# Fifteen seven-product pairs in each half of a down projection, with one weight sum of each fresh pair formed by GpSimd

## The chip, the core and the metric

The kernel runs on one core of one Trainium2 chip. The time is the device time of one execution in microseconds (us). Five engines work side by side, each on its own list of instructions in a fixed order: TensorE (PE in the profile), VectorE (DVE), ScalarE (ACT), GpSimd (POOL) and SyncE (SP), whose list here holds transfers only. GpSimd's list holds both computing and the start of transfers. An instruction that waits holds up everything behind it on its own list.

## The reference, cut to what matters

```python
def reference(x, ...):                       # x: (1, 256, 2048) float32, one layer
    x = mixer_block(x, ...)                  # gated token mixer, unchanged by this edit
    x = conv_ffn(x, norm_ffn, w_up, conv_k, conv_b, w_down)
    return rms_norm(x, norm_final)

def conv_ffn(x, g_norm, w_up, conv_k, conv_b, w_down):
    up = rms_norm(x, g_norm) @ w_up          # 2048 -> 2 x 5504 columns
    up = ...                                 # width-3 convolution over positions
    gate, val = jnp.split(up, 2, axis=-1)
    return x + (jax.nn.silu(gate) * val) @ w_down   # 5504 -> 2048: the down projection
```

The edit concerns the last product, a (256 x 5504) matrix times a (5504 x 2048) matrix, and a little of the final norm.

## The kernel before, in words

**Precision.** A float32 number is used as a high part plus a low part. Each product of two blocks is three matmuls: high x high, low x high, high x low. The function `triple` issues them on lines 323, 324 and 325, in this order. The high part of a weight block is made by ScalarE (`whi`, line 176), the low part by VectorE (`wlo`, line 177), both from the raw block that a transfer brought (`wraw`, five buffers, issued on SyncE's list from line 148). `whi` and `wlo` have four buffers each.

**Tiling of the down projection.** The 2048 output columns are done in two halves of 1024, which the text calls the first and the second half. In each half the 5504 inner rows are 43 blocks of 128, so 21 pairs of blocks and one single block. One block times 1024 columns is a piece. The 256 positions are two halves of 128, the columns of a piece two halves of 512, and a pair therefore is a 2 x 2 block product: eight triples, or, by the Strassen-Winograd scheme, seven. The list `DOWN_PAIRS` names the pairs of rows that go the second way, and `DOWN_QUADS` the places (0 to 20) in each half's order at which they stand. The text calls these places q0 to q20; place q has pieces 2q and 2q+1. There are three kinds of pair:

- a plain pair: eight triples on the split raw blocks, four per piece;
- a fresh pair: seven triples, three in its first piece and four in its second. Its second piece needs four sums of raw weight blocks, in the tiles t13 and t24 (two sums each), and their high and low parts h13, l13, h24, l24. They are made on the spot: `weight_sums` forms the sums on VectorE (lines 366, 367, 369, 370), and `weight_sums_split` the parts (line 380 on ScalarE, line 381 on VectorE). Each tile exists once, so a pair's parts can be written only when TensorE has done with those of the fresh pair before;
- a read pair (`DOWN_SPLIT`, five of the list): seven triples, whose parts were made and written to DRAM during the up projection by `split_ahead`, and are read back (`split_read`, line 1274) on GpSimd's list into tiles of the pool "twice".

Both kinds of seven-product pair also need sums of activations. They are formed during the up projection (`sums`, `sums_split` in `ev_up`, lines 1113 to 1117), written to DRAM, and read back by `stored` (line 1420) on GpSimd's list into three tiles in turn; each read waits until TensorE has done with the pair three places earlier in that turn.

**Order of the work.** `begin(i)` stands ahead of the matmuls of piece i. It issues loads up to piece i+4, splits up to piece i+3, and runs what `at(i, ...)` put there: for a fresh pair at piece i the sums at i-3 and their parts at i-2. So VectorE and ScalarE run up to three pieces ahead of TensorE, and the buffers hold them there.

**The end.** The last four pieces of the second half are done block by block of the output (`finish`), so that the norm of one block overlaps the products of the next. `ev_sums` adds the seven-product terms to the residual stream a little earlier; its last two adds are lines 1010 and 1011.

In the trace all of t13, t24, h13, h24, l13, l24 and two of the three tiles of `stored` have the name h, and the third has the name s; ff's activations are a. TensorE's weight side and moving side are both listed, so `bank<-h,h` is a product with sums of weights.

Of the kernel before, what the change touches and what calls it, by code (L numbers as in the profile page):

```python
# [69 lines left out]
PAD = 16  # L70
DOWN_PAIRS = (2, 3, 5, 6, 7, 9, 10, 11, 13, 14, 15, 16, 17, 18)
DOWN_QUADS = ((1, 3, 5, 6, 7, 9, 10, 11, 13, 14, 15, 17, 18, 19), (1, 2, 4, 5, 6, 8, 9, 10, 12, 13, 14, 16, 17, 18))
DOWN_SPLIT = (2, 6, 10, 14, 17)
DOWN_JOBS = ((0, 2), (4, 6), (8, 10), (12, 14), (16, 18))
DOWN_LEADS = ({2: (4, 16, 16), 3: (5,), 5: (8,), 6: (7, 8, 8)}, {})
TWICE_AT = -15
SCALE_AT = (14, 15, 22, 23)
FIN_AT = 36


@with_exitstack
def trunk_kernel(ctx, tc, x, x_t, vecs, w_in, ln_g, ln_b, w_st, b_s, rpb, w_branch, w_out, w_up, w_down,
# [108 lines left out]

    tasks = {}
    preload = {}

# [94 lines left out]

    def wide(src, row0, order, c0, acts, quads, room, done, sums=None, stored=None, split=None, late=False, lead=4, behind=(), ahead={}):  # L290
        n0 = plan_wide(src, row0, order, c0)
        boxes = {}
        for q in quads:
            i = n0 + 2 * q
            k = order[2 * q]
            units[i], units[i + 1] = 1, 2
            b = boxes[q] = {}
            ready = split[0].get(k // 2) if split else None
            if stored:
                b["acts"] = {}  # L300
                at(i - (ready[0] if ready else ahead.get(k // 2, lead)), lambda b=b, k=k: stored(k // 2, b["acts"]))
            else:
                b["acts"] = sums[k]
            if ready:
# [4 lines left out]
            whole[i] = whole[i + 1] = None  # L309
            halves = late and q == quads[0]  # L310
# [48 lines left out]

    def weight_sums(i, box, room, halves=False):  # L360
        r0, r1 = whole.pop(i), whole.pop(i + 1)
# [7 lines left out]
        nc.vector.tensor_add(t13[:, 0], r0[:, 0], r0[:, 1])  # L369
        nc.vector.tensor_add(t13[:, 1], r0[:, 1], r1[:, 1])  # L370
        if halves:
# [3 lines left out]

    def weight_sums_split(box, room):
        u = []
        for name, t in zip(("13", "24"), box.pop("w")):
            h, l = room("h" + name, F32R), room("l" + name, F32R)
            nc.scalar.activation(h, t, AF.Copy)  # L380
            nc.vector.tensor_sub(l, t, h.bitcast(F32))
            u.append((h, l))
        split_sums(box, u)

# [4 lines left out]
    def run_wide(g, tail=0):  # L389
# [20 lines left out]
        for i in range(n0, n1 - tail):  # L410
# [30 lines left out]
            if sp:  # L441
                done[0](P, i)
        if not tail:
            done[1](C, n1)
            return
# [544 lines left out]

    def ev_sums(j, room):
        def done(P, i):
# [172 lines left out]
    def finish(ps, t, c):  # L1165
        x2 = rs["x2"]
        last = t == NT - 1 and c == 1
        if c == 0:
            fin["y", t] = hpool.tile([128, 2, 512], F32, name=f"h{t}")
        y, g = fin["y", t], fin["g", 2 + c]  # L1170
        if last:
            square_columns(t, 2 + c, ps[t][c])
        else:
            add_down(ps[t][c], t, 2 + c)
            square_columns(t, 2 + c)
            nc.vector.tensor_mul(y[:, c], columns_of(t, 2 + c), g)
        if c == 0:
            if t:
                fin["out"]()
            else:  # L1180
                p = ps[NT - 1][1]
                nc.vector.tensor_add(p, p, columns_of(NT - 1, 3))
# [240 lines left out]

    def down_split_tile(pair, name):
        return ff["twice"].tile([128, 2, 512], F32R, name=name)

    d_kept = {}

    def down_order(g):
# [4 lines left out]

    g_dn = [wide(w_d, 0, down_order(g), g * 1024, lambda k: ff["a"][k], DOWN_QUADS[g], down_room,
                 (ev_sums(2 * g, down_room), ev_down if g == 0 else finish), stored=stored,
                 ahead={p: n[0] for p, n in DOWN_LEADS[g].items()},
                 split=({p: DOWN_LEADS[g].get(p, (6, 6)) for p in DOWN_SPLIT}, split_read(d_kept, g, down_split_tile))) for g in range(2)]
    ff["kept"] = {p: dram.tile([128, 2, 384], F32, name=f"sums{p}") for p in DOWN_PAIRS}
# [120 lines left out]

    at(g_dn[0][1] + TWICE_AT, open_twice)
    at(g_dn[0][1] + 3, open_third)
    for g in g_up:
        run_group(g)

    def open_fin():
        fc["st"].close()
        fin["p"], fin_st = pool("fin", "right")
# [4 lines left out]
    fin["ss"] = const.tile([128, NT, 4], F32, name="ss_3")  # L1573
    at(g_dn[0][1] + FIN_AT, open_fin)
    def load_fin():
# [49 lines left out]
```

## Time and profile before

| | |
|---|---|
| time, median of 3 runs | 1286.87 us (1286.46 to 1287.11) |
| the profiled execution | 1286.83 us |
| its span, first to last instruction | 1285.0 us, so 1.8 us lie around it |
| granted TensorE clock, mean | 0.998 |
| busy: TensorE, VectorE, ScalarE, GpSimd | 99%, 88%, 62%, 14% of the span |
| the down projection's products | 1061 to 1276.6 us of the span |

The profiled execution stands 0.04 us below the median, well inside the runs' spread of 0.65 us. TensorE's busy time is made of matmuls whose ends are modelled, so 99% says that it never lacked work for long, and nothing of how fast it worked; for that the starts of successive matmuls have to be looked at.

### The profile page before, as it was taken

What the parts mean: (1) busy time and instruction counts of PE and PEld (TensorE: products, weight loads), DVE (VectorE), ACT (ScalarE), POOL (GpSimd) and SP (SyncE); (2) the same over time, 40 slices, a digit from 0 to 9 for tenths busy, and PEclk for the clock granted to TensorE, in tenths of its full rate; (3) what the DMA queues carried; (4) which work ended last, traced back from release to release, by engine and by line L of the source; (5) the groups of instructions that cost most, each with busy time, mean ns of one, the idle gap of its engine ahead of it and who ended that gap; (6) DMA issues with size and microseconds to landing.
All of it is one profiled execution on the core that took longest, in us unless ns stands there. A gap on an engine that the chain in (4) does not pass through costs nothing.

```text
span 1285.0 us, 19798 instructions
## 1 busy us (share of the span) xinstructions
PE 1275.2 (99%) x6711; PEld 1088.0 (85%) x6711; DVE 1128.0 (88%) x1675; ACT 795.9 (62%) x1198; POOL 174.4 (14%) x328
## 2 busy tenths in 40 slices
PE   9999999999999999999999999999999999999997
PEld 7888888888888888888888888888888888888886
DVE  7898977777799988897989999899999989989988
ACT  7776575775755555566656666566566656555554
POOL 0003842330000001100000010011001001211210
PEclk9999999999999999999999999999999999999999
DMA  9779889989789967965878888888788779998993
GB/s 365 279 271 278 289 270 345 333 288 323 255 310 368 351 234 255 390 219 180 278 239 258 298 268 259 280 287 273 247 300 290 250 252 341 359 384 337 370 373 144
DMA packets 200485, 375.54 MB, mean 292 GB/s; under 512 B 16320, under 2 KB 124480, under 8 KB 200384
## 3 DMA queue, kind: packets, MB, share of 16 engines
q1 hardware_dynamic: 175472, 285.84, 64.1%
q0 software_dynamic: 24480, 87.78, 19.5%
q8 instruction: 52, 0.85, 0.3%
q10 hardware_dynamic: 432, 0.66, 0.1%
q14 instruction: 49, 0.40, 0.1%
HBM read 323.63 MB, written 48.50 MB: 290 GB/s over the span
## 4 chain that ended last, share of the span: by engine, by line
PE 96%; DVE 2%; DMA 1%; issue 0%; ACT 0%; DVEq 0%; SPq 0%; ACTq 0%
PE bank L228 31%; PE bank L232 16%; PE bank L323 11%; PE bank L325 11%; PE bank L324 11%; PE bank L256 5%; PE bank L257 5%; PE bank L258 5%; DMA wraw<-in_w_down_dram 1%; DVE wlo L177 0%; PE bank L877 0%; PE bank L831 0%; PE bank L504 0%; PE bank L866 0%; PE bank L704 0%
## 5 line engine op out<-in xcount | busy, mean ns | idle before, releaser
L177 DVE TENSOR_TENSOR wlo<-wraw,whi 128x1024 fp32r<-128x1024 f32 (+1 forms) x471 | 534.8, 1150 | 113.1 <-ACT whi L176 73.8
L176 ACT ACTIVATE whi<-wraw 128x1024 fp32r<-128x1024 f32 (+1 forms) x471 | 460.3, 993 | 219.3 <-PE bank L324 65.4
L228 PE MATMUL bank<-h,whi 128*128 128x512 f32 x1760 | 423.3, 391 | 0.0
L228 PEld LDWEIGHTS bank<-h,whi 128*128 128x128 f32 x1760 | 322.8, 188 | 62.0
L232 PEld LDWEIGHTS bank<-h,wlo 128*128 128x128 f32 x1760 | 225.9, 191 | 8.7
L232 PE MATMUL bank<-h,wlo 128*128 128x256 f32 x1760 | 228.6, 283 | 0.0
L1088 ACT ACTIVATE tc<-ta,ck 128x256 f32<-128x256 f32 x86 | 47.1, 595 | 106.6 <-DVE ta L1086 106.6
L325 PE MATMUL bank<-wlo,a 128*128 128x512 f32 x200 | 78.0, 390 | 0.0
L324 PE MATMUL bank<-whi,a 128*128 128x512 f32 x200 | 77.8, 389 | 0.0
L323 PE MATMUL bank<-whi,a 128*128 128x512 f32 x200 | 77.8, 389 | 0.0
L323 PE MATMUL bank<-whi,h 128*128 128x512 f32 x168 | 66.0, 393 | 0.0
L324 PE MATMUL bank<-whi,h 128*128 128x512 f32 x168 | 65.6, 390 | 0.0
L325 PE MATMUL bank<-wlo,h 128*128 128x512 f32 x168 | 65.5, 390 | 0.0
L1091 DVE SCALAR_TENSOR_TENSOR tc<-ta,ck,tc 128x255 f32<-128x255 f32 x86 | 41.4, 482 | 14.4 <-ACT tc L1088 14.4
L1314 DVE TENSOR_TENSOR tw<-tw 128x512 f32<-128x512 f32 x72 | 50.3, 699 | 0.7
L256 PE MATMUL bank<-whi,h 128*128 128x512 f32 x128 | 50.3, 393 | 0.0
L256 PE MATMUL bank<-whi,y 128*128 128x512 f32 x128 | 50.3, 393 | 0.0
L257 PE MATMUL bank<-whi,h 128*128 128x512 f32 x128 | 49.8, 389 | 0.0
L257 PE MATMUL bank<-whi,y 128*128 128x512 f32 x128 | 49.8, 389 | 0.0
L258 PE MATMUL bank<-wlo,h 128*128 128x512 f32 x128 | 49.8, 389 | 0.0
L258 PE MATMUL bank<-wlo,y 128*128 128x512 f32 x128 | 49.8, 389 | 0.0
L380 ACT ACTIVATE h<-h 128x1024 fp32r<-128x1024 f32 x36 | 38.0, 1057 | 16.5 <-DVE h L370 13.7
(329 smaller groups left out, 1988.8 us busy)
## 6 DMA issues: line engine op xcount, KB each, us to landing
wraw<-in_w_up_dram SPq DMA_DIRECT2D x336, 256.0 KB, 4.2
wraw<-in_w_in_dram SPq DMA_DIRECT2D x107, 512.0 KB, 6.3
wraw<-in_w_down_dram SPq DMA_DIRECT2D x76, 512.0 KB, 7.5
wraw<-in_w_in_dram SPq DMA_DIRECT2D x70, 256.0 KB, 4.4
wraw<-in_w_branch_dram SPq DMA_DIRECT2D x32, 512.0 KB, 5.4
wraw<-in_w_out_dram SPq DMA_DIRECT2D x28, 512.0 KB, 6.8
tw<-in_w_down_dram POOLq DMA_DIRECT2D x10, 1024.0 KB, 8.0
down_h<-so POOLq DMA_DIRECT2D x20, 512.0 KB, 3.7
```

The source lines that it names most:

```text
L176: nc.scalar.activation(h[:, k, :m], w[:, k, :m], AF.Copy)
L177: nc.vector.tensor_sub(l[:, k, :m], w[:, k, :m], h[:, k, :m].bitcast(F32))
L228: nc.tensor.matmul(p, h[:, k - k0, b * 128:(b + 1) * 128], acts(k), start=k == 0, stop=k == nk - 1)
L232: nc.tensor.matmul(p[:, :T], l[:, k - k0, b * 128:(b + 1) * 128], acts(k)[:, 0, :], start=False, stop=False)
L256: nc.tensor.matmul(p, xh, h[:, kk, :m], start=st, stop=False)
L257: nc.tensor.matmul(p, xl, h[:, kk, :m], start=False, stop=False)
L258: nc.tensor.matmul(p, xh, l[:, kk, :m], start=False, stop=sp)
L323: nc.tensor.matmul(p, xh, h, start=st, stop=False, **kw)
L324: nc.tensor.matmul(p, xl, h, start=False, stop=False, **kw)
L325: nc.tensor.matmul(p, xh, l, start=False, stop=sp, **kw)
L1088: nc.scalar.activation(v, u, AF.Identity, scale=ck[:, 1, ch:ch + 1], bias=ck[:, 3, ch:ch + 1])
L1314: nc.vector.tensor_add(w[:, d], w[:, a], w[:, b])
```

## The change

The list of seven-product pairs grows from fourteen to fifteen (pair 12 is new), in both halves. Pair 11 takes the place of pair 10 among the five that are read; so ten pairs instead of nine are fresh in each half. With fewer plain pairs to stand between, two fresh pairs follow each other directly at two places of each half: q9 and q10, q16 and q17 in the first; q8 and q9, q15 and q16 in the second. For the second pair of three of these four (`DOWN_BESIDE`) h13 and l13 get tiles of their own, in a pool opened where the convolution's was, or in activation tiles that the second half no longer needs (`DOWN_FREED`); the rest of their parts, and at q17 of the first half all of them, are issued behind the products of the piece before (`after`). Pair 17's h13 and l13 are read into such tiles too.

In the down projection `weight_sums` now gives the sum t13[:, 1] of each fresh pair to GpSimd. The last two adds of the second half's `ev_sums` move into `finish`. The pool for the final norm opens 49 - 36 = 13 pieces later (the first half has 43 pieces, and it now opens at piece 6 of the second), and two scalings move from pieces 22 and 23 to 24 and 25.

```diff
-DOWN_PAIRS = (2, 3, 5, 6, 7, 9, 10, 11, 13, 14, 15, 16, 17, 18)
+DOWN_PAIRS = (2, 3, 5, 6, 7, 9, 10, 11, 12, 13, 14, 15, 16, 17, 18)
...
-DOWN_SPLIT = (2, 6, 10, 14, 17)
+DOWN_SPLIT = (2, 6, 11, 14, 17)
...
+DOWN_BESIDE = ((10,), (9, 16))
+DOWN_FREED = ((0, 2), (1, 3))
...
-            at(i - 3, lambda i=i, b=b, halves=halves: weight_sums(i, b, room, halves))
+            at(i - 3, lambda i=i, b=b, halves=halves: weight_sums(i, b, room, halves, nc.gpsimd if helped else nc.vector))
...
+            if q in beside:
+                at(i - 2, lambda b=b, q=q: weight_sums_split(b, room, (0,), beside[q]))
+                after[i - 1] = lambda b=b: weight_sums_split(b, room, (1,))
+                continue
+            if q - 1 in made:
+                after[i - 1] = lambda b=b: weight_sums_split(b, room)
+                continue
...
         nc.vector.tensor_add(t13[:, 0], r0[:, 0], r0[:, 1])
-        nc.vector.tensor_add(t13[:, 1], r0[:, 1], r1[:, 1])
+        second.tensor_add(t13[:, 1], r0[:, 1], r1[:, 1])
...
             def second_half():
                 nc.vector.tensor_sub(x12, x12, m["v"])
+                if last:
+                    fin["x21"] = lambda: nc.vector.tensor_add(x21, x21, m["u3"])
+                    fin["x22"] = lambda: nc.vector.tensor_sub(x22, x22, m["w"])
+                    return
...
     def finish(ps, t, c):
...
             square_columns(t, 2 + c)
+            if (t, c) == (0, 1):
+                fin["x21"]()
             nc.vector.tensor_mul(y[:, c], columns_of(t, 2 + c), g)
...
+                fin["x22"]()
                 p = ps[NT - 1][1]
```

VectorE's list in the first half, before, around the fresh pairs at q15 (tiles h_11980, h_11981) and q17 (h_12065, h_12066); L369, L370, L366, L367 are the four sums, L381 the two low parts:

```order
L370 TENSOR_TENSOR h_11980<-wraw 128x512
L366 TENSOR_TENSOR h_11981<-h_11980,wraw 128x512
L367 TENSOR_TENSOR h_11981<-wraw,h_11981 128x512
L177 TENSOR_TENSOR wlo<-wraw,whi 128x1024
L381 TENSOR_TENSOR h_12005<-h_11980,h_12004 128x1024
L381 TENSOR_TENSOR h_12009<-h_11981,h_12008 128x1024
L177 TENSOR_TENSOR wlo<-wraw,whi 128x512
L177 TENSOR_TENSOR wlo<-wraw,whi 128x1024
L177 TENSOR_TENSOR wlo<-wraw,whi 128x512
L369 TENSOR_TENSOR h_12065<-wraw 128x512
L370 TENSOR_TENSOR h_12065<-wraw 128x512
L366 TENSOR_TENSOR h_12066<-h_12065,wraw 128x512
```

The same list now, around the neighbours q16 (h_12132, h_12133) and q17 (h_12187, h_12188); L379, L376, L377 are the three sums left, L392 the low parts, L178 `wlo`:

```order
L377 TENSOR_TENSOR h_12133<-wraw,h_12133 128x512
L178 TENSOR_TENSOR wlo<-wraw,whi 128x1024
L392 TENSOR_TENSOR h_12161<-h_12132,h_12160 128x1024
L392 TENSOR_TENSOR h_12165<-h_12133,h_12164 128x1024
L178 TENSOR_TENSOR wlo<-wraw,whi 128x512
L379 TENSOR_TENSOR h_12187<-wraw 128x512
L376 TENSOR_TENSOR h_12188<-h_12187,wraw 128x512
L377 TENSOR_TENSOR h_12188<-wraw,h_12188 128x512
L178 TENSOR_TENSOR wlo<-wraw,whi 128x1024
L178 TENSOR_TENSOR wlo<-wraw,whi 128x512
L392 TENSOR_TENSOR h_12243<-h_12187,h_12242 128x1024
L392 TENSOR_TENSOR h_12247<-h_12188,h_12246 128x1024
```

One sum of four is gone from each pair, the whole pair in between is gone, and the second pair's low parts stand behind the splits of two more pieces.

GpSimd's list at the same place, before; L1420 reads activation sums, L1274 the parts of a read pair:

```order
L1420 DMA h_12012<-sums_168 128x768
L1420 DMA h_12097<-sums_169 128x768
L1420 DMA s_12132<-sums_170 128x768
L1274 DMA h_12134<-down_h_17_0_204 128x1024
L1274 DMA l_12135<-down_l_17_0_205 128x1024
L1274 DMA h_12138<-down_h_17_0_206 128x1024
L1274 DMA l_12139<-down_l_17_0_207 128x1024
```

And now, with the sums L380 for q14 (h_12045), q16 (h_12132) and q17 (h_12187) among the reads (L1441 and L1295):

```order
L380 TENSOR_TENSOR h_12045<-wraw 128x512
L1441 DMA h_12077<-sums_169 128x768
L1441 DMA s_12115<-sums_170 128x768
L380 TENSOR_TENSOR h_12132<-wraw 128x512
L1295 DMA hx<-down_h_17_0_205 128x1024
L1295 DMA lx<-down_l_17_0_206 128x1024
L1295 DMA h_12168<-down_h_17_0_207 128x1024
L1295 DMA l_12169<-down_l_17_0_208 128x1024
L380 TENSOR_TENSOR h_12187<-wraw 128x512
```

Each sum now stands behind reads that wait for TensorE: q16's behind the read of sums_170, whose tile the pair at q14 used, and q17's behind the read into h_12168, whose tile the read pair at q15 used.

More of the change, by code (lines that the diff above doesn't have):

```diff
@@ L285, in run_group, with wide @@
             done(ps, b)
-    def wide(src, row0, order, c0, acts, quads, room, done, sums=None, stored=None, split=None, late=False, lead=4, behind=(), ahead={}):
+    def wide(src, row0, order, c0, acts, quads, room, done, sums=None, stored=None, split=None, late=False, lead=4, behind=(), ahead={}, beside={}, helped=False):
         n0 = plan_wide(src, row0, order, c0)
-        boxes = {}
+        boxes, made = {}, set()
         for q in quads:
@@ L1422, in stored, with freed, extra, beside @@
         box["s"].append((fourth(pair, 0), fourth(pair, 1)))
-    def down_split_tile(pair, name):
-        return ff["twice"].tile([128, 2, 512], F32R, name=name)
+    def freed(pair):
+        return ff["ap"][pair].rearrange("p a b t -> p a (b t)")
+    def extra(name):
+        return ff["extra"].tile([128, 2, 512], F32R, name=name)
+    def beside(g):
+        return lambda: tuple(extra(n) if g == 0 else freed(p) for n, p in zip(("hx", "lx"), DOWN_FREED[0]))
+    def down_split_tile(g):
+        def tile_of(pair, name):
+            if pair == DOWN_SPLIT[-1] and name in ("h13", "l13"):
+                return extra(name[0] + "x") if g == 0 else freed(DOWN_FREED[1][name == "l13"])
+            return ff["twice"].tile([128, 2, 512], F32R, name=name)
+        return tile_of
     d_kept = {}
```

46 lines of the change are left out of this document (28 added, 18 removed).

## The prediction

> **What bounds the kernel now.** I read the page first, then the starts of single matmuls, then VectorE's and GpSimd's timelines in the down projection.
>
> ```profile
> span 1285.0 us, 19798 instructions
> PE 96%; DVE 2%; DMA 1%; issue 0%; ACT 0%; DVEq 0%; SPq 0%; ACTq 0%
> 1060.00:1276.60 216.60, 216.60 (x958) 178.75 (x957) 198.08 (x252) 122.91 (x151) 35.63 (x67) 1.00 0.88 333
> ```
>
> The third row is a table by stretches: TensorE, weight loads, VectorE, ScalarE, GpSimd, clock, transfers' share, GB/s. The chain that ended last is TensorE, and in the down projection TensorE is never idle while VectorE (198.08 of 216.60 us) is not far below. Busy does not tell TensorE's speed; successive starts do.
>
> ```profile
> 1267.64 0.39 PE L323 MATMUL bank<-h,a 128*128 128x512 f32 x1
> ...
> 1276.25 0.39 PE L325 MATMUL bank<-l,a 128*128 128x512 f32 x1
> ```
>
> These two rows are 38 steps apart (39 matmuls follow each other without a gap), so a step is 8.61 / 38 = 0.2266 us; the 0.39 is the length of one, of which most overlaps the next. The stage has 948 such matmuls (per half 14 x 21 + 7 x 24 + 12 = 474), and 948 x 0.2266 = 214.8 us of the 216.6. It runs at TensorE's step throughout. So only fewer matmuls can save time here, and anything that makes TensorE wait adds.
>
> **What VectorE has to do, and how far ahead it is.** One fresh pair (q9, first half):
>
> ```profile
> 1101.46 0.69 DVE L369 TENSOR_TENSOR h<-wraw 128x512 f32<-128x512 f32 x1
> 1102.06 0.69 DVE L370 TENSOR_TENSOR h<-wraw 128x512 f32<-128x512 f32 x1
> 1102.66 0.69 DVE L366 TENSOR_TENSOR h<-h,wraw 128x512 f32<-128x512 f32 x1
> 1103.38 0.69 DVE L367 TENSOR_TENSOR h<-wraw,h 128x512 f32<-128x512 f32 x1
> 1103.99 1.22 DVE L177 TENSOR_TENSOR wlo<-wraw,whi 128x1024 fp32r<-128x1024 f32 x1
> 1105.13 2.36 DVE L381 TENSOR_TENSOR h<-h,h 128x1024 fp32r<-128x1024 f32 x2
> 1107.40 0.68 DVE L177 TENSOR_TENSOR wlo<-wraw,whi 128x512 fp32r<-128x512 f32 x1
> ...
> 1109.20 0.39 PE L323 MATMUL bank<-h,h 128*128 128x512 f32 x1
> ```
>
> By starts, four sums take 1103.99 - 1101.46 = 2.53 us (0.63 each), a full split 1.14, the two low parts 2.27, and with a half split of 0.60 a fresh pair costs VectorE 6.54 us, a plain pair 2 x 1.14 = 2.28, a read pair 0.60 + 1.14 = 1.74. TensorE takes 21 x 0.2266 = 4.76 us for a seven-product pair and 5.44 for a plain one. So VectorE loses 1.78 us of lead at a fresh pair and wins some 3 at the others. The slack of q9 is the time from the end of l13 (1105.13 + 1.22 = 1106.35) to the third matmul of the triple, which is the first to read it (1109.20 + 2 x 0.2266 = 1109.65): 3.30 us. It is least at the start of the stage:
>
> ```profile
> 1078.02 2.36 DVE L381 TENSOR_TENSOR h<-h,h 128x1024 fp32r<-128x1024 f32 x2
> 1079.28 0.39 PE L323 MATMUL bank<-h,h 128*128 128x512 f32 x1
> ...
> 1084.96 0.69 DVE L370 TENSOR_TENSOR h<-wraw 128x512 f32<-128x512 f32 x1 [1.11 <-DMA wraw<-in_w_down_dram]
> ...
> 1088.04 2.35 DVE L381 TENSOR_TENSOR h<-h,h 128x1024 fp32r<-128x1024 f32 x2
> 1089.48 0.39 PE L323 MATMUL bank<-h,h 128*128 128x512 f32 x1
> ```
>
> At q3 it is 1079.73 - 1079.24 = 0.49 us, at q5 1089.93 - 1089.26 = 0.67.
>
> **The change, part by part.** *The new pair:* three matmuls less in each half, 6 x 0.2266 = 1.36 us off TensorE. The bound is exact, since no step is shorter.
>
> *The GpSimd sum.* The trace of before has no add on GpSimd. Its nearest rows are the masks' selects, which read one operand, beside VectorE:
>
> ```profile
> 176.69 0.72 POOL L795 TENSOR_SCALAR_AFFINE_SELECT bias<-bias 64x512 f32<-64x512 f32 x1
> 177.45 1.08 POOL L795 TENSOR_SCALAR_AFFINE_SELECT bias<-run 64x128 f32<-64x128 f32 x4
> 178.60 1.57 POOL L795 TENSOR_SCALAR_AFFINE_SELECT bias<-bias 64x512 f32<-64x512 f32 x1
> ...
> 178.35 1.25 DVE L177 TENSOR_TENSOR wlo<-wraw,whi 128x1024 fp32r<-128x1024 f32 x1 [2.69 <-ACT whi L176]
> ...
> 138.84 1.40 DVE L693 TENSOR_TENSOR ta<-bank,tb 128x256 f32<-128x256 f32 x4
> ...
> 140.17 1.70 DVE L675 TENSOR_TENSOR ta<-ta,rb 128x256 f32<-128x256 f32 x4
> ...
> 143.02 1.91 DVE L1314 TENSOR_TENSOR tw<-tw 128x512 f32<-128x512 f32 x2
> ...
> 140.19 1.85 POOL L795 TENSOR_SCALAR_AFFINE_SELECT bias<-run 64x128 f32<-64x128 f32 x4
> 142.10 1.57 POOL L795 TENSOR_SCALAR_AFFINE_SELECT bias<-bias 64x512 f32<-64x512 f32 x1
> ```
>
> A select of 512 elements takes 0.72 us while VectorE idles (the 2.69 us ahead of 178.35), and 1.57 when it meets a VectorE split: it waits until that ends. VectorE pays too: four operations with one operand in PSUM take 1.40 beside GpSimd, four of the same size with both in SBUF 1.70; and two 512-wide sums, 0.63 + 0.69 = 1.32 elsewhere, take 1.91. Of that 0.59, some 0.09 is a short select (0.30 over the three or four beside the 1.70) and 0.50 the long one: VectorE loses what GpSimd's instruction takes less 0.22. The Trainium skill's page "SBUF — State Buffer", section "Who interferes with whom", says the same: a VectorE instruction with two SBUF inputs contends with a GpSimd instruction that reads SBUF, one blocking the other for its whole length. All VectorE work around the moved sum has two SBUF inputs, so this rule speaks against the move.
>
> The add reads two operands. By the selects' slope, (0.72 - 0.27) / 384 = 1.17 ns per element with 0.12 fixed, two operands in turn give 0.12 + 2 x 0.60 = 1.32 us, my value; the low end is 0.72 (both at once), the high end 1.57 + 1.57 = 3.14. VectorE then loses 1.32 - 0.22 = 1.10 us and saves 0.63: 0.47 worse per fresh pair, between 0.13 better and 2.29 worse. (By the skill's page "GPSIMD Engine Reference", section "Performance versus the Vector engine", an add of 2048 elements takes 4497 ns, so estimated 1.12 us for 512; with it the net is 0.27 and the stalls below fall to about 0.1 us.) The sum over a half is no bound: 10 x 7.01 + 5 x 1.74 + 6 x 2.28 + 1.14 = 93.6 us against 471 x 0.2266 = 106.7. Places decide.
>
> *Early places.* At q3 0.47 is just covered by 0.49; at q5 twice that, 0.94, meets 0.67: a stall of up to 0.27, less if VectorE's wait for weights there (1.11 us ahead of 1084.96) absorbs some. I take 0.2.
>
> *Neighbours.* From l13 of one to l13 of the next VectorE needs 7.01 us where TensorE takes 4.76. At q9 the slack of 3.30 has shrunk by four shifts (1.88, partly absorbed) to about 2.0, and 2.25 goes: 0.2 of stall. At q17 of the first half the sum is held in another way. GpSimd's list makes an add wait behind reads, and reads wait for TensorE:
>
> ```profile
> POOL h L1420 <- PE bank L325: 112.8, 16, 17.8
> 1136.18 0.54 POOL L1420 DMA_DIRECT2D s<-sums  x1 [4.21 <-PE bank L325]
> 1136.71 0.53 POOL L1274 DMA_DIRECT2D h<-down_h  x1
> ...
> L380 ACT ACTIVATE h<-h 128x1024 fp32r<-128x1024 f32 x36 | 38.0, 1057 | 16.5 <-DVE h L370 13.7
> ```
>
> The waits row says how often: 112.8 us in 16 waits. The add for q16 stands behind such a read, which starts when TensorE ends q14. From that moment: read 0.54, wait for a VectorE operation and add to about 2.4, high part (1.05) to 3.5, l13 4.6, l24 5.8, half split 6.4, three sums and the second add 9.4, two splits 11.1, l13 of q17 12.3. TensorE reads it after q15, q16 and half of q17, 2 x 4.76 + 9 x 0.2266 + 0.45 = 12.0: stall 0.2 or so. In the second half one neighbour has a tile of its own and comes out 0 to 0.3 ahead, the other has slack over. Sum of stalls: 0.2 + 0.2 + 0.2 = 0.6, of which I take 0.5.
>
> *Transfers.* Two more reads of 384 KB:
>
> ```profile
> l<-down_l POOLq DMA_DIRECT2D x18, 512.0 KB, 9.3
> h<-sums POOLq DMA_DIRECT2D x18, 384.0 KB, 6.0
> DMA to landing us min/median/max: 4.2/8.5/13.2
> ```
>
> They are issued pieces ahead, as now, and cost nothing while that holds. The tight one is h24, l24 of pair 17: they start when TensorE ends q15 (first half) or q14 (second) and are needed 51 steps, 6 more and 2 for the low part later, 13.4 us, against a median of 9.3 plus 1.1 for two issues of 0.53 and a largest of 13.2. Zero, or 0.9 if the largest falls there; I take zero.
>
> *Up projection.* The new pair's activation sums add to VectorE four 128-wide operations, one 384-wide and one 128-wide, 5 x 0.29 + 0.55 = 2.0 us:
>
> ```profile
> L1115 DVE TENSOR_TENSOR so<-sw,so 128x384 fp32r<-128x384 f32 x6 | 3.3, 553 | 0.0
> L329 DVE TENSOR_TENSOR sw<-tc 128x128 f32<-128x128 f32 x6 | 1.7, 287 | 0.0
> 900.00:950.00 50.00, 50.00 (x289) 44.21 (x288) 46.55 (x84) 31.52 (x51) 3.96 (x7) 1.00 0.85 283
> ```
>
> Here later groups carry both these sums and a split job with TensorE at 50.00 of 50.00, while the group that gets pair 12's sums has no job. Nothing.
>
> *The end.* Two adds of 0.63 us move behind the first output block:
>
> ```profile
> 1274.77 0.68 DVE L1130 TENSOR_TENSOR x<-bank,x 128x512 f32<-128x512 f32 x1
> 1276.74 0.60 ACT L1136 ACTIVATE junk<-bank 128x512 f32<-128x512 f32 x1
> ```
>
> VectorE's total before the third block's add is unchanged, and the last chain starts from ScalarE's square right after TensorE's last matmul. Nothing.
>
> **Sum.** 1286.83 - 1.36 + 0.5 = 1285.97 for the profiled execution, which stood at the median: 1286.0.
>
> **Rivals.** (A) As above, stalls of 0.1 to 1.2 us: 1285.6 to 1286.7. For it: the slack rows and the selects.
> (B) The add costs VectorE less than it saves, so nothing stalls: 1286.83 - 1.36 = 1285.5. For it: the low end of 0.72; against it: VectorE's 1.70 against 1.40.
> (C) Slower: the add is longer than estimated and VectorE falls behind at the neighbours. Each 0.1 us more costs 0.2 at each of four neighbour places and at q5, 1.0 in all, less a few tenths of slack in the second half. From an add of about 1.7 us the kernel is over 0.2% slower; at 2.0 it is 1286 + 6 = 1292. For it: the add is the one unmeasured price, and a GpSimd operation meeting VectorE took 1.57; against it: the slope.
> (D) Reads or loads land late, as transfers are busy 0.88 of the stage and more of it with two reads added: one or two stalls of 0.9 and some from fresh weights behind the held sums, 1286.7 to 1288.8, which eats the gain.
>
> **How the numbers follow.** A 0.60, B 0.14, C 0.13, D 0.13. 0.2% is 2.6 us, about what a measurement of this kernel tells from no change. A, B and nearly all of D lie inside it; the most that TensorE can give back is 1.36, so faster needs something unseen, 0.02. Slower: C but for its mildest part, and a little of D, 0.12. Same 0.86. Range: B's lower edge with the runs' spread of 0.3, 1285.2, to the upper edge of D, 1288.8.
>
> **What would show it.** Right: 942 matmuls of the stage at a step of 0.227, TensorE's gaps under 1.2 us in all and at q5, q10 and q17; GpSimd's adds 1.3 us where VectorE idles and up to 2.5 where not; VectorE operations beside them 1.0 to 1.1 longer. Wrong: adds above 1.7 us, gaps of whole microseconds at neighbours, or gaps ended by transfers.

## Result and the profile after

The kernel after takes 1295.91 us (median of 6, 1294.52 to 1298.38) against 1286.95 (6 runs, 1286.46 to 1287.26) for the kernel before: ratio 1.0071, 95% interval 1.0058 to 1.0084. It is 9.0 us slower, and outside the range given. The profiled execution took 1298.38 us, the slowest of the six, so the trace shows 11.6 us of span more than before, some 2.5 above the median.

The page of the kernel after:

```profile
span 1296.6 us, 19869 instructions
PE 1279.3 (99%) x6705; PEld 1087.9 (84%) x6705; DVE 1146.3 (88%) x1673; ACT 798.2 (62%) x1204; POOL 212.2 (16%) x351
PE 91%; DMA 3%; DVE 3%; issue 1%; POOL 0%; ACT 0%; DVEq 0%; POOLq 0%; SPq 0%; ACTq 0%
L380 POOL TENSOR_TENSOR h<-wraw 128x512 f32<-128x512 f32 x20 | 37.2, 1861 | 82.1 <-DMA wraw<-in_w_down_dram 69.0
```

The last row is the GpSimd sum: 20 of them, 1.86 us each with the waits inside it. In the chain that ended last TensorE falls from 96% to 91%. TensorE still shows 99% busy: neither that share nor VectorE's 88% gives the loss away. The waits of the down projection do (us in total, times, longest):

```profile
PE bank L335 <- DVE wlo L178: 6.1, 5, 2.2
POOL h L380 <- DMA wraw<-in_w_down_dram: 69.0, 12, 13.1
SPq L149 <- DVE wlo L178: 110.9, 58, 3.8
SPq L149 <- POOL h L380: 18.9, 9, 3.4
```

TensorE waits five times for `wlo`, the low part of a raw block; for a sum's low part it waited 0.25 us at most. Measured from start to start, less the step of 0.2266, the five are 0.65 us (q3, first half), 0.61 (q10, first half), 2.20 (q17, first half), 2.33 (q9, second half) and 1.10 (q16, second half), 6.89 in all. The last two rows belong to the transfers' list: loads of raw blocks wait for VectorE's splits, as before, and now for GpSimd too.

The longest wait but one, on TensorE's timeline:

```profile
1148.91 0.39 PE L334 MATMUL bank<-whi,a 128*128 128x512 f32 x1
1151.34 0.50 PE L335 MATMUL bank<-wlo,a 128*128 128x512 f32 x1 [2.04 <-DVE wlo L178]
...
1154.10 0.63 PE L334 MATMUL bank<-h,s 128*128 128x512 f32 x1
1154.52 0.63 PE L335 MATMUL bank<-h,s 128*128 128x512 f32 x1
...
1156.16 0.39 PE L333 MATMUL bank<-h,a 128*128 128x512 f32 x1
1156.38 0.39 PE L334 MATMUL bank<-h,a 128*128 128x512 f32 x1
```

After the wait the matmuls start 0.42 to 0.43 us apart instead of 0.23, for some 3 us: the wait is paid twice. The same in a table by stretches, whose third column from the end is the granted clock:

```profile
1149.24:1152.65 3.41, 1.37 (x7) 1.05 (x6) 3.38 (x5) 3.02 (x4) 0.00 (x0) 1.00 1.01 404
1152.65:1156.06 3.41, 3.41 (x9) 2.40 (x8) 3.41 (x5) 0.14 (x1) 0.00 (x0) 0.50 1.01 417
1220.92:1224.33 3.41, 1.47 (x6) 1.24 (x7) 3.41 (x5) 2.79 (x4) 0.54 (x1) 1.00 1.03 423
1224.33:1227.74 3.41, 3.41 (x9) 2.67 (x8) 3.41 (x5) 0.55 (x1) 0.52 (x1) 0.50 0.98 364
```

Behind the two longest waits the clock stands at 0.50 for 3.41 us, which costs 1.75 and 1.59 us (the starts' excess over 0.2266), 3.3 together. One such stretch lowers the mean granted clock of an execution by 0.0013 (1.7 of 1296.6 us). Three of the six executions have a mean of 0.998, as the kernel before, and took 1294.52 to 1295.08 us; those at 0.996 and 0.995 took 1296.74 to 1298.38. So the halving seems to be missing in half of the executions, and without it the kernel is still 7.6 us or more slower.

The end grew as well. The rows that answer to TensorE's last matmul and ScalarE's square behind it:

```profile
1286.73 0.39 PE L335 MATMUL bank<-l,a 128*128 128x512 f32 x1
...
1286.34 0.68 DVE L1148 TENSOR_TENSOR x<-bank,x 128x512 f32<-128x512 f32 x1
...
1288.30 0.57 ACT L1154 ACTIVATE junk<-bank 128x512 f32<-128x512 f32 x1
```

The square stands 1.57 us behind the start of the last matmul, where it stood 0.49 behind (1276.74 and 1276.25), because VectorE comes late: its add for the third block started 1.48 us ahead of the last matmul (1274.77) and now starts 0.39 ahead.

The sum: -1.36 for six matmuls, +6.89 of waits, +3.34 of halved clock, +0.96 of small gaps beyond the 0.25 of before, +1.08 at the end, +0.40 because the stage began later in this execution (at the same gap 1064.60 against 1064.20) = 11.3 of 11.6.

### The profile page after: what moved, and what is told of

Same layout as the page of the kernel before. It is cut to its first block, busy times and chain, and to the rows that moved or that the text cites. A ratio compares the mean times of both kernels' runs of the same rounds, so it can differ in the third digit from the quotient of the medians.

```text
span 1296.6 us, 19869 instructions
## 1 busy us (share of the span) xinstructions
PE 1279.3 (99%) x6705; PEld 1087.9 (84%) x6705; DVE 1146.3 (88%) x1673; ACT 798.2 (62%) x1204; POOL 212.2 (16%) x351
## 4 chain that ended last, share of the span: by engine, by line
PE 91%; DMA 3%; DVE 3%; issue 1%; POOL 0%; ACT 0%; DVEq 0%; POOLq 0%; SPq 0%; ACTq 0%
PE bank L230 31%; PE bank L234 16%; PE bank L335 10%; PE bank L333 9%; PE bank L334 9%; PE bank L258 5%; PE bank L260 4%; PE bank L259 4%; DMA wraw<-in_w_down_dram 3%; DVE wlo L178 1%; DMA s<-xsums 1%; POOL h L380 0%; PE bank L891 0%; PE bank L845 0%; PE bank L518 0%
## 5 line engine op out<-in xcount | busy, mean ns | idle before, releaser
L178 DVE TENSOR_TENSOR wlo<-wraw,whi 128x1024 fp32r<-128x1024 f32 (+1 forms) x471 | 540.9, 1162 | 103.4 <-ACT whi L177 65.0
L335 PE MATMUL bank<-wlo,a 128*128 128x512 f32 x190 | 74.7, 393 | 6.1 <-DVE wlo L178 6.1
L333 PE MATMUL bank<-whi,a 128*128 128x512 f32 x190 | 74.0, 389 | 0.0
L334 PE MATMUL bank<-whi,a 128*128 128x512 f32 x190 | 74.0, 389 | 0.0
L391 ACT ACTIVATE h<-h 128x1024 fp32r<-128x1024 f32 x37 | 38.4, 1056 | 23.6 <-DVE h L379 11.6
L380 POOL TENSOR_TENSOR h<-wraw 128x512 f32<-128x512 f32 x20 | 37.2, 1861 | 82.1 <-DMA wraw<-in_w_down_dram 69.0
```

What stands on the lines that cost most here:

```text
L178: nc.vector.tensor_sub(l[:, k, :m], w[:, k, :m], h[:, k, :m].bitcast(F32))
L333: nc.tensor.matmul(p, xh, h, start=st, stop=False, **kw)
L334: nc.tensor.matmul(p, xl, h, start=False, stop=False, **kw)
L335: nc.tensor.matmul(p, xh, l, start=False, stop=sp, **kw)
```

## The experiments

Each was timed against the kernel before on the same chip, which stood at 1286.97 to 1287.01.

**All four sums on VectorE.** GpSimd forms nothing; pairs, order and tiles are as after.

```diff
-                 beside={q: beside(g) for q in DOWN_BESIDE[g]}, helped=True) for g in range(2)]
+                 beside={q: beside(g) for q in DOWN_BESIDE[g]}) for g in range(2)]
```

> The changed kernel with all four sums of each fresh pair on VectorE again; the fifteen pairs, their order and tiles stay. Theory 1 (the add on GpSimd takes 1.1 us of VectorE and gives back 0.63): VectorE regains about 0.5 us at each of 20 fresh pairs, TensorE's gaps of 11.4 us (half-clock stretches counted in) shrink below 4, time 1286 to 1289 us. Theory 2 (the neighbouring fresh pairs alone are too much for VectorE): gaps stay at 8 us or more, no granted clock below full is avoided, 1293 us or more. Theory 3 (GpSimd holds the raw weights' buffers, so loads start late): as theory 1 in time, but the loads' starts move forward by the time that SyncE now waits for GpSimd's adds.

1287.33 us, ratio 1.0002 (0.9992 to 1.0011). Of the 9.0 us, 8.6 hang on who forms the one sum. The order is not free either: the six matmuls saved do not show. The page's busy times:

```profile
PE 1274.6 (99%) x6705; PEld 1086.3 (84%) x6705; DVE 1137.1 (88%) x1693; ACT 801.0 (62%) x1204; POOL 175.8 (14%) x331
```

VectorE is busy 1137.1 us with 20 operations more than after, where it was 1146.3: moving 20 sums away from it made it 9.2 us busier. On TensorE's timeline one wait is left, at q9 of the second half, 1.47 us from start to start:

```profile
1216.14 0.50 PE L335 MATMUL bank<-wlo,a 128*128 128x512 f32 x1 [1.30 <-DVE wlo L178]
```

**The sum on GpSimd in the kernel before.** No new pair, no neighbours; 18 sums.

```diff
-        nc.vector.tensor_add(t13[:, 1], r0[:, 1], r1[:, 1])
+        second.tensor_add(t13[:, 1], r0[:, 1], r1[:, 1])   # second: GpSimd in the down projection
```

> The kernel before, fourteen pairs in its own order, with the same one sum of each of its 18 fresh pairs given to GpSimd. Theory 1: VectorE is 0.5 us worse per fresh pair, which shows only where the slack is under 0.5 us: gaps of 0.3 to 1.0 us at the first two fresh pairs, none later, 1287 to 1288.5 us. Theory 2: no gap beyond those of before, 1287.0. Theory 3: late loads show as ScalarE waiting longer for weights throughout, 1289 or more.

1289.37 us, ratio 1.0020 (1.0010 to 1.0029): 2.4 us for 18 sums, beyond the 1287 to 1288.5 of theory 1 and inside theory 3's "1289 or more". TensorE's waits grew to 2.2 us, the longest 0.84 at q3, and the time from the last matmul's start to the end from 8.80 to 10.25 us. The sign of theory 3 came in part: in the down projection ScalarE waited 36.0 us for raw weights where it had waited 28.3, and loads waited 19.7 us for GpSimd's sums. The page's busy times:

```profile
PE 1275.8 (99%) x6711; PEld 1087.1 (84%) x6711; DVE 1135.7 (88%) x1657; ACT 795.8 (62%) x1198; POOL 206.7 (16%) x346
```

VectorE, with 18 operations fewer, is 7.7 us busier than before (1128.0).

**A GpSimd operation of the same size that nothing waits for**, in the kernel before, at the same 18 places.

```diff
+            if idle_sum:
+                at(i - 3, lambda: nc.gpsimd.tensor_sub(junk, junk, junk))
```

> The kernel before with an extra GpSimd subtraction of 128x512 on a scratch tile at the place of each fresh pair's sums, 18 in all; it holds no weights and its result is not used. Theory 1: VectorE operations that meet it are 1.1 us longer (total VectorE busy up by up to 20 us), nothing is given back, gaps at the first fresh pairs and perhaps one later, 1287.5 to 1290 us. Theory 3: it holds no buffer, so the time is that of before, 1287.0. Theory 2: 1287.0.

1289.35 us, ratio 1.0017 (1.0007 to 1.0026). It holds no weight buffer and nothing needs its result, yet it costs as much as the sum. So reading alone has a price. The page:

```profile
PE 1275.8 (99%) x6711; PEld 1088.2 (85%) x6711; DVE 1143.2 (89%) x1675; ACT 797.1 (62%) x1198; POOL 198.3 (15%) x346
```

VectorE has the same 1675 operations as before and is busy 1143.2 us instead of 1128.0: 0.84 us lost to each of the 18. That is 15.2 us more, against 7.7 with the sum, for the same time: VectorE's busy time alone does not set the price, and these two runs leave open how much of the sum's 2.4 us is what it holds up, the loads and ScalarE. The operation itself, in the table by groups of the down projection:

```profile
L315 POOL TENSOR_TENSOR junk<-junk 128x512 f32<-128x512 f32 x18 | 23.3, 1296 | 0.8 <-ACT junk L1138 0.4
```

Its mean of 1.30 us includes what it waited for VectorE.

**The same, with a GpSimd operation that reads nothing.**

```diff
-                at(i - 3, lambda: nc.gpsimd.tensor_sub(junk, junk, junk))
+                at(i - 3, lambda: nc.gpsimd.memset(junk, 0.0))
```

> The kernel before plus a GpSimd operation at each of the 18 made-on-the-spot pairs, three pieces ahead, as in the run with the subtraction beside; here it is a memset of the same 128x512 tile, which writes and reads nothing. Theory (GpSimd and VectorE shut each other out only while GpSimd reads): VectorE's busy time in the stage stays within 2 us of the 198.5 before, its operations beside a memset keep their 0.69, and the time is that of before, 1286.7 to 1287.3. Rival (any GpSimd work at these places costs, by its semaphores, its writes or what its queue holds up): the 2.3 us of the subtraction again, 1289.0 to 1289.6.

1287.14 us, ratio 1.0001 (0.9992 to 1.0010). The page:

```profile
PE 1275.4 (99%) x6711; PEld 1087.6 (85%) x6711; DVE 1127.5 (88%) x1675; ACT 796.0 (62%) x1198; POOL 185.7 (14%) x346
```

VectorE stays at 1127.5 against 1128.0. The fill, in the table by groups:

```profile
L315 POOL MEMSET junk<- 128x512 f32 x18 | 9.8, 546 | 0.0
```

So it is GpSimd's reading that VectorE pays for, not its writing, its semaphores or its list. The page "SBUF — State Buffer" of the Trainium skill, section "Who interferes with whom", draws the line there: a VectorE instruction with two SBUF inputs contends with a GpSimd instruction that reads SBUF, "not with one that only writes it". Both halves of that sentence agree with these runs.

**The kernel after with GpSimd filling the place of the sum.** A memset writes the same tile at the same place and is waited for as before; the sum itself is left out.

```diff
-        second.tensor_add(t13[:, 1], r0[:, 1], r1[:, 1])
+        if second is nc.gpsimd:
+            second.memset(t13[:, 1], 0.01)
+        else:
+            second.tensor_add(t13[:, 1], r0[:, 1], r1[:, 1])
```

> The kernel after, but GpSimd fills the second half of t13 with a constant (a memset) where it formed the sum b1 + d1: it writes the same tile at the same place and is waited for as before, and reads nothing; the sum itself is left out, so the output is not the reference's. Theory (what the GpSimd sum costs is what its reading takes from VectorE, nothing else): VectorE's busy time in the stage falls below the 205.2 of all sums on VectorE by 20 operations, to 191 to 195, no wait of TensorE over 0.5 us, no halved clock, the end as short as before, and the time is that of the change's six matmuls fewer: 1285.4 to 1286.0, ratio 0.9988 to 0.9993. Rival (the waits come from the order of the work and from what waits for GpSimd: ScalarE for the finished sum, the loads for its release): waits at q17 of the first half and q9 and q16 of the second again, 1289 or more.

1286.09 us, ratio 0.9992 (0.9983 to 1.0001): the 9 us are gone, and of the 1.36 us of the six matmuls 0.9 show, with an interval that holds the whole and just reaches no change. The page:

```profile
PE 1274.4 (99%) x6705; PEld 1086.0 (84%) x6705; DVE 1127.2 (88%) x1673; ACT 799.2 (62%) x1204; POOL 187.8 (15%) x351
```

VectorE's 1673 operations take 1127.2 us; in the kernel after the same 1673 took 1146.3. That is 19.1 / 20 = 0.96 us lost per sum. On TensorE's timeline two waits over 0.5 us stayed, 1.26 and 0.62, both ended by reads and not by VectorE; the longer:

```profile
1257.92 0.50 PE L335 MATMUL bank<-l,h 128*128 128x512 f32 x1 [1.10 <-DMA l<-down_l]
```

The longer one is the read of l24 of pair 17. The memset also doesn't hold the raw blocks as the sum does. So the 9 us go with a GpSimd operation that reads the raw blocks; how much of them is VectorE's lost time and how much the late release of those blocks, no run here parts.

**The sum on GpSimd away from the neighbours only (twelve), and at the neighbours only (eight).**

```diff
+            near = q in near_quads                  # the other kernel: not in
-            at(i - 3, lambda i=i, b=b, halves=halves: weight_sums(i, b, room, halves, nc.gpsimd if helped else nc.vector))
+            at(i - 3, lambda i=i, b=b, halves=halves, near=near: weight_sums(i, b, room, halves, nc.gpsimd if helped and not near else nc.vector))
...
+                 ... near_quads=((9, 10, 16, 17), (8, 9, 15, 16))[g]) for g in range(2)]
```

> The kernel after, but in the four pairs of neighbours (q9, q10 and q16, q17 of the first half; q8, q9 and q15, q16 of the second) all four sums are on VectorE; the other 12 made-on-the-spot pairs keep the GpSimd sum. Theory (the GpSimd sum costs little where one made-on-the-spot pair stands alone and much where two stand in a row, since there VectorE has no idle time to give): 1287.3 with all sums on VectorE, plus 12/18 of the 2.4 us that 18 such sums cost in the kernel before, 1.6: 1288.9, between 1288.0 and 1289.7; no wait above 2 us, no halved clock. Rival (the 8.6 us are spread over all 20 sums, 0.43 each): 1287.3 + 12 x 0.43 = 1292.5.

> The kernel after with the GpSimd sum in the four pairs of neighbours alone (eight sums); the other twelve made-on-the-spot pairs have all four sums on VectorE. Theory (the waits at the neighbours are made by their own sums, which run while VectorE has no idle time): waits of TensorE at q17 of the first half and q9 and q16 of the second half above 1 us, at least one of them long enough to halve the clock, and an end as short as with all sums on VectorE: 1287.3 plus 5 to 8: 1292.3 to 1295.3. Rival (the twelve and the eight add up to the twenty: 1295.9 - (1291.35 - 1287.33)): 1291.9. Second rival (the waits at the neighbours come from lateness that the other twelve sums leave behind): under 1290.

The twelve: 1291.35 us, ratio 1.0033 (1.0019 to 1.0046), 4.0 above all sums on VectorE. The interval, 1289.5 to 1292.9, leaves out the 1288.9 of the theory and holds the 1292.5 of its rival. The waits grew by 1.4 us (0.68 at q3, 1.03 and 0.69 at q9 and q16 of the second half, against the one of 1.47), and the end by 1.8. The eight: 1292.99 us, ratio 1.0044 (1.0031 to 1.0058), 5.7 above. With 4.0 + 5.7 = 9.7 against 8.6 for all twenty, and intervals of 1.7 us to each side, they add up within the error. So by the medians a sum at a neighbour costs about twice one elsewhere (0.7 us against 0.33), and "little elsewhere" was wrong. The eight do give long waits at the neighbours:

```profile
1149.86 0.50 PE L336 MATMUL bank<-wlo,a 128*128 128x512 f32 x1 [1.39 <-DVE wlo L178]
...
1220.09 0.50 PE L336 MATMUL bank<-wlo,a 128*128 128x512 f32 x1 [2.24 <-DVE wlo L178]
```

No halved clock followed in this execution, not even behind the 2.24; the run with VectorE held, below, says why. The end, held to stay short, was 0.9 us longer (9.58 against 8.68).

**One sum alone on GpSimd**, that of the last fresh pair, q18 of the second half.

```diff
+                 ... near_quads=((), (18,))[g]) for g in range(2)]     # GpSimd there, VectorE elsewhere
```

> The kernel after with all fourth sums on VectorE but one: that of the last made-on-the-spot pair, q18 of the second half, stays on GpSimd. Theory (behind that pair VectorE has no idle time up to the last output, since it converts the last pieces ahead of TensorE and then runs the end's operations from a full queue; so what the GpSimd sum takes from it there, 1.0 to 1.5 us, shows whole at the end): last matmul as with all sums on VectorE, the time from the last matmul to the end 1.0 to 1.5 us longer, 1287.3 plus that: 1288.3 to 1288.8. Rival (a sum costs the mean of the twenty, 8.6 / 20 = 0.43 us, wherever it stands): 1287.8. Second rival (the late end came from lateness gathered over the whole half): 1287.3 and an end as long as before.

1287.66 us, ratio 1.0004 (0.9995 to 1.0013). In the profile the last matmul's start to the end took 9.35 us instead of 8.68, and the time 0.33 us more than with all on VectorE, which the intervals do not separate from nothing or from 0.43. The 1.0 to 1.5 of the theory did not come. What made the end 1.8 us longer with the twelve sums is not settled: this one pair gives at most a part. Up to this one sum the program is that with all sums on VectorE, yet its wait at q9 of the second half is 0.56 us where it was 1.47. So a single wait can differ by 0.9 us from one profile to the next with nothing changed ahead of it.

**Where the scalings stand.** After with the first two scalings later:

```diff
-SCALE_AT = (14, 15, 24, 25)
+SCALE_AT = (20, 21, 24, 25)
```

> The changed kernel with the first two scalings of the final norm (two VectorE operations of 0.68 us) moved from pieces 14 and 15 of the second half, where the second of two neighbouring fresh pairs is prepared, to pieces 20 and 21, a read pair. If that neighbour's gap (2.33 us, then 1.7 lost at half clock) comes from VectorE being about 1.2 us too late there: the gap falls to about 1 us and no half clock follows, 1292 to 1293.5 us. If the neighbours' order or late weights decide it: 1295.5 to 1297 as measured.

1294.37 us, ratio 1.0059 (1.0042 to 1.0076). The wait at q9 of the second half fell from 2.33 to 0.79 us and its halved clock went; but q16 went from 1.10 to 2.27. The time lies between the two ranges. In one profile each, moving the scalings takes 1.5 us off that wait, and VectorE's lateness moves on to the next neighbours. The same move with all sums on VectorE:

```diff
-SCALE_AT = (14, 15, 24, 25)       # all sums on VectorE
+SCALE_AT = (20, 21, 24, 25)
```

> The kernel after with all four sums on VectorE and the two scalings of x2 moved from pieces 14 and 15 of the second half to 20 and 21. Theory (without the GpSimd sum the one wait left, 1.47 us at q9 of the second half, came from the two scalings that stand in VectorE's queue between the neighbours' operations): that wait falls under 0.3 us, nothing new of more than 0.4 us at q16, so 1287.3 less 1.2 to 1.5: 1285.6 to 1286.2, ratio 0.999 to the kernel before. Rival (the neighbours overrun VectorE by themselves, the scalings only meet it): the wait stays above 1 us or moves to q16, and the time stays at 1287.0 to 1287.6.

1287.85 us, ratio 1.0004 (0.9995 to 1.0013): the 1.47 us wait went, and waits for `wlo` of 0.70 (q17, first half) and 0.55 (q16, second half) came, with one of 0.75 (q17, second half) that the read of l24 of pair 17 ended. All scalings late:

```diff
-SCALE_AT = (14, 15, 24, 25)       # all sums on VectorE
+SCALE_AT = (24, 25, 36, 37)
```

> The kernel after with all four sums on VectorE and all scalings of x2 late in the second half: the first two at pieces 24 and 25, where the second two stood, those at 36 and 37. Theory (the one wait left with all sums on VectorE, 1.47 us at q9 of the second half, is the two scalings ahead of it; the leads that VectorE had at pieces 24 to 27 and from 38 on, 2 us and more, take two scalings each): no TensorE wait over 0.4 us, 1287.3 less 1.2 to 1.5: 1285.8 to 1286.2, ratio 0.9990 to 0.9994. Rival (the neighbours overrun VectorE by themselves, or the late scalings lengthen the end): 1286.9 to 1287.8.

1287.39 us, ratio 1.0002 (0.9994 to 1.0011). TensorE does run through: no wait above 0.36 us. The last matmul starts 1.15 us earlier than with the scalings in their place (1276.92), and the end takes it back:

```profile
1275.77 0.39 PE L335 MATMUL bank<-l,a 128*128 128x512 f32 x1
...
1277.30 0.57 ACT L1154 ACTIVATE junk<-bank 128x512 f32<-128x512 f32 x1
```

The square stands 1.53 us behind the last matmul, as in the kernel after. With all sums on VectorE its list is nearly a second limit: work taken out of TensorE's way stands in the way of the end. No kernel that computes everything came out measurably faster than before.

**When the clock halves.** The kernel before, VectorE held at four places:

```diff
+    def hold(n):
+        for _ in range(n):
+            nc.vector.tensor_sub(junk, junk, junk)
+    for i, n in ((g_dn[0][1] + 24, 8), (g_dn[1][1] + 6, 14), (g_dn[1][1] + 14, 11), (g_dn[1][1] + 22, 9)):
+        at(i, lambda n=n: hold(n))
```

> The kernel before, with VectorE held by 8, 14, 11 and 9 idle subtractions of a 128x512 tile (about 0.69 us each by the trace of before) issued at four places of the down stage, so that TensorE waits there for its low parts for different times. Theory (each long wait also halves TensorE's clock): every wait above 2.2 us, the shortest that did it in the kernel after, is followed within 4 us by a granted clock of 0.5 for 3.41 us, where a step is 0.427 us instead of 0.227, so that 1.7 to 2 us more are lost; waits up to 1.5 us show none of it. Rival (the halving after those two waits was by chance or from the load of the chip): waits of 2.5 us and more without it, or a halved clock after short ones.

1309.32 us, a single run. Waits of 0.75, 6.70, 3.17 and 2.88 us from start to start; the clock halved behind the last three, for 6.83, 3.41 and 6.83 us. In the two that lasted twice as long, TensorE was busy 1.99 and 2.84 us of the first 3.41 at the halved clock; in the other it was busy 3.07. The table by stretches, with the first and the last of them:

```profile
1194.80:1198.21 3.41, 1.71 (x8) 1.09 (x6) 3.24 (x6) 1.06 (x1) 0.54 (x1) 1.00 0.65 214
1198.21:1201.63 3.42, 0.00 (x0) 0.00 (x0) 3.28 (x5) 0.00 (x0) 0.00 (x0) 1.00 0.02 9
1201.63:1208.46 6.83, 5.41 (x13) 4.20 (x14) 6.76 (x11) 2.13 (x3) 0.00 (x0) 0.50 0.53 166
...
1249.42:1252.83 3.41, 1.18 (x6) 0.64 (x4) 3.31 (x6) 1.06 (x1) 0.54 (x1) 1.00 0.60 219
1252.83:1259.66 6.83, 6.26 (x14) 4.47 (x15) 6.76 (x12) 2.17 (x3) 0.54 (x1) 0.50 0.66 223
```

All its changes of clock lie on one grid of 3.413 us (from 1208.46 to 1228.94 and from 1232.35 to 1252.83 it is six of them). With that grid laid over the run with the eight sums, from a change behind its last matmul, the 2.24 us wait falls into two cells:

```profile
1215.36:1218.77 3.41, 2.49 (x11) 1.71 (x10) 3.34 (x6) 1.83 (x3) 0.57 (x1) 1.00 1.03 419
1218.77:1222.19 3.42, 2.10 (x9) 1.76 (x10) 3.42 (x5) 2.28 (x3) 0.54 (x1) 1.00 1.04 417
```

The rule of the expectation (length of the wait) was too simple: a cell in which TensorE is busy 1.47 us or less of 3.41 is followed by a halved one (1.37 and 1.47 above, 1.18 and 0.00 here), one with 1.71, 2.10 or 2.49 is not. In the run with one sum alone a cell of 1.57 us (1275.56 to 1278.97, the last matmuls) is not followed by a halved one either.

## Why the prediction was wrong, by its own steps

*Right.* TensorE's part: the page counts six matmuls fewer (6705 for 6711), and where the sum costs VectorE nothing the time is 0.9 us lower (1286.09), within its error of 1.36. The price of the sum, too. A meeting in the kernel after in which GpSimd comes first:

```profile
1093.74 1.30 POOL L380 TENSOR_TENSOR h<-wraw 128x512 f32<-128x512 f32 x1
...
1093.77 1.83 DVE L379 TENSOR_TENSOR h<-wraw 128x512 f32<-128x512 f32 x1
```

GpSimd takes 1.30 us where it comes first (estimated 1.32), and VectorE's 0.68 becomes 1.83. Over the trace VectorE lost 0.96 us per sum (1.10 forecast), and against having all four sums it is 9.2 / 20 = 0.46 us busier per fresh pair (0.47 forecast).

*Failed: "sum of stalls 0.2 + 0.2 + 0.2, of which I take 0.5".* The same 0.47 that was priced rightly gave 6.89 us of waits. q3 was held to be just covered and waited 0.65; q5 was given 0.2 and did not wait; q10 was given 0.2 and waited 0.61. All five waits are for `wlo`, the full split of a fresh pair's second piece, and the prediction took its slacks from l13. In the kernel before, at q3:

```profile
1076.88 1.22 DVE L177 TENSOR_TENSOR wlo<-wraw,whi 128x1024 fp32r<-128x1024 f32 x1
...
1078.35 0.40 PE L325 MATMUL bank<-wlo,a 128*128 128x512 f32 x1
```

The split ends at 1078.10 and is read at 1078.35: a slack of 0.25 us, where l13 has 0.49. The large waits are the three other neighbours. At q17 of the first half:

```profile
1138.27 0.54 POOL L1441 DMA_DIRECT2D s<-sums  x1 [7.30 <-PE bank L335]
1140.67 1.77 POOL L380 TENSOR_TENSOR h<-wraw 128x512 f32<-128x512 f32 x1 [1.86 <-DMA wraw<-in_w_down_dram]
...
1140.60 0.69 DVE L376 TENSOR_TENSOR h<-h,wraw 128x512 f32<-128x512 f32 x1 [1.62 <-DMA wraw<-in_w_down_dram]
1141.33 1.67 DVE L377 TENSOR_TENSOR h<-wraw,h 128x512 f32<-128x512 f32 x1
...
1146.32 1.77 DVE L178 TENSOR_TENSOR wlo<-wraw,whi 128x512 fp32r<-128x512 f32 x1
...
1150.07 1.82 DVE L178 TENSOR_TENSOR wlo<-wraw,whi 128x1024 fp32r<-128x1024 f32 x2
```

The walk started at 1138.27 and put the end of l24 at 5.8 us, and the full split of q17's second piece, after three sums and the add, at some 10.5. It came at 13.0 (1151.29 on the trace, from 1150.07 + 1.22). Of the 2.5 us, 1.8 had come by the end of GpSimd's first sum (4.2 us after the start instead of 2.4), mostly by its 1.86 of wait for raw weights; most of the rest is what VectorE lost to that sum (1.67 at 1141.33 instead of 0.69). The wrong reader counts here too: the walk asked when l13 is read, while the full split is read first, by the sixth matmul of the pair, due at 1149.14, 10.9 us after the start. By the walk's own numbers that left 0.4 us.

*Failed: "transfers: nothing".* It counted the two added reads and took the weights as landed. But loads wait for buffers that VectorE's splits and GpSimd's sums free (the two rows of the transfers' list above). The load that was late here, in the kernel after behind GpSimd's sum for q14, then with all sums on VectorE:

```profile
1128.04 2.42 POOL L380 TENSOR_TENSOR h<-wraw 128x512 f32<-128x512 f32 x1 [1.93 <-DMA wraw<-in_w_down_dram]
...
1130.48 0.33 SPq L149 DMA_DIRECT2D wraw<-in_w_down_dram  x1
```

```profile
1126.52 0.33 SPq L149 DMA_DIRECT2D wraw<-in_w_down_dram  x1
```

In the kernel after the profile puts its wait down to that sum; in both it landed some 10 us after its start. A late sum means late loads, and so VectorE waiting for weights at the very place where it should catch up. ScalarE's high part of that piece, in the same two kernels:

```profile
1140.61 1.06 ACT L177 ACTIVATE whi<-wraw 128x1024 fp32r<-128x1024 f32 x1 [2.96 <-DMA wraw<-in_w_down_dram]
```

```profile
1136.78 1.07 ACT L177 ACTIVATE whi<-wraw 128x1024 fp32r<-128x1024 f32 x1 [1.73 <-DMA wraw<-in_w_down_dram]
```

The same weights come 3.8 us later in the one than in the other. Of this 0.45 is the later start of the stage and some 1.6 what TensorE had waited before (q3, q10 and small gaps, which the other does not have); about 1.7 us are late against TensorE. This is the chain of rival D behind the cause of rival C, which the prediction kept apart. The tight read, h24 and l24 of pair 17 ("Zero, or 0.9 if the largest falls there; I take zero"), cost the kernel after no wait of TensorE above 0.2 us; but it ended waits of 1.26, 0.75 and 0.61 us in three other kernels with fifteen pairs (GpSimd filling; all sums on VectorE with two scalings moved; the eight sums).

*Failed: the second half's "0 to 0.3 ahead" and "slack over".* It left out two scalings that stand in VectorE's list between the neighbours:

```profile
1216.63 1.78 DVE L1158 TENSOR_TENSOR x<-x,gfin 128x512 f32<-128x512 f32 x1
...
1220.99 0.68 DVE L1158 TENSOR_TENSOR x<-x,gfin 128x512 f32<-128x512 f32 x1
1221.59 1.22 DVE L178 TENSOR_TENSOR wlo<-wraw,whi 128x1024 fp32r<-128x1024 f32 x1
```

The split for which TensorE waited 2.33 us stands right behind the second; the first was stretched to 1.78 by a sum. With both moved away the wait was 1.5 us shorter.

*Left out: the clock.* In the profiled execution 3.3 us followed the two longest waits. The walk counted a wait as its own length.

*Failed: "the end: nothing".* The two moved adds cost nothing by themselves: with all sums on VectorE the end took 8.68 us against 8.80 before. But VectorE reached that work later than TensorE needed it: 1.08 us. The run with the late scalings shows the same lengthening (1.53 against 1.57 behind the last matmul) with no GpSimd sum at all; there two scalings stand late in VectorE's list. So the end has no room for VectorE's lateness, whatever makes it.

Rival C had the direction (VectorE falls behind at the neighbours) with a wrong condition: it asked for a sum of 1.7 us or more when alone. At 1.30 us it was already true, because C's slope counted each place's delay once, without the loads and the clock. How much of the 9.0 us each link of the chain gives (VectorE's lost time, the late loads) stays open; that the sum on GpSimd carries 8.6 of them is shown.

## What to carry to other kernels

Work moved from VectorE to GpSimd is not taken off VectorE if GpSimd reads SBUF beside VectorE operations with two SBUF inputs: here VectorE got 0.46 us busier per sum that it no longer formed, while a fill of the same size cost it nothing. A slack of a few tenths at one instruction is no cover when buffers tie the loads to the late engine: walk every reader of every tile up to the next load, and take in everything that stands in that engine's list. A wait of TensorE that left it busy 1.47 us or less of one 3.41 us cell of the clock's grid cost some 1.6 us or more on top of its length.

## What the runs showed of the hardware that was not expected

The clock of TensorE was halved in units of 3.41 us on a free-running grid: a cell busy 1.47 us or less was followed by a halved one, a cell busy 1.57 or more was not (the eight cells above). So the same wait costs its length or 1.6 to 1.8 us more by where it falls: 2.20 us at q17 of the kernel after did halve the clock, 2.40 in the run with eight sums (2.24 of it idle) did not. The page "TensorE: Matmul & The Clock Gate" of the Trainium skill, section "What's actually happening", gives the window as free-running and 3413 ns long, which the grid here confirms. It has the clock fall back after at least one idle window; here a window 57% idle (1.47 us busy of 3.41) was enough.
